# A decoder step whose three inner norms are applied after the first products of the next projection, and whose last two down groups are multiplied together

## The chip, the cores and the metric

One core of one Trainium2 chip runs one inference step of a two-layer decoder. The metric is the device time of one execution in microseconds; lower is better. All numbers are fp32; products run as pairs of `float32r` halves (below).

## The reference, cut to what matters

320 tokens (256 of a prompt, 64 of eight samples) pass through two layers of width 2048. Layer 0 has sparse attention with its own K/V, layer 1 dilated attention on a K/V that is projected once from the output of layer 0. After each mixer and each ConvFFN stands a layer norm over the 2048 features:

```python
x = LN(ALPHA * x + mixer(x))                # norm 1 (layer 0), norm 3 (layer 1)
x = LN(ALPHA * x + conv_ffn(x))             # norm 2 (layer 0), the output norm (layer 1)

def layer_norm(x, g, b):
    mu = x.mean(-1); var = square(x - mu).mean(-1)
    return (x - mu) * rsqrt(var + EPS) * g + b

def conv_ffn(h, state, w_up, conv_w, conv_b, w_down):
    gate, up = split(h @ w_up)              # 2048 -> 2 x 5504
    conv = conv_b + sum(ext[:, j:j + T] * conv_w[j] for j in range(3))
    return (silu(conv) * up) @ w_down       # 5504 -> 2048
```

What follows norms 1 and 3 is `h @ w_up`; what follows norm 2 is the shared `h @ w_kv` and then the query projection of layer 1. The change is about these three norms; the output norm isn't touched.

## The kernel before

**Layout.** Activations lie transposed: 16 tiles of 128 features (`d` = 0 to 15) by 320 tokens. R holds the residual, one `big` buffer of 128 x 5120; four such buffers exist.

**Products.** `Stream` walks one long list of weight chunks (4 feature tiles by 256 columns, 512 KB). Of each it issues the load on SP's queue three chunks ahead, splits it into `hi` on ScalarE (L82) and `lo` on VectorE (L84), two chunks ahead of use, and multiplies: for each feature tile three products of 128 x 128 weights by 320 columns, `hi*xh`, `hi*xl`, `lo*xh` (L123 to L125), accumulating in PSUM over 16 feature tiles. So a chunk of two column tiles is 24 products. A job is one or two column blocks; when a block is done its epilogue `epi_*` is called. Between chunks the `lanes` hand out steps of side work (attention, norms, tables) at given rates. The Tile scheduler then orders each engine's instructions, except those pinned by `keep_in_program_order`.

**The order of jobs.** ... wo of layer 0 (`epi_wo` adds each block to R, L502), the FFN, the shared K/V (`kvb`, `vb`), 24 query blocks (`qb`) with the attention of layer 1 beside them, wo of layer 1, the second FFN. An FFN works in groups of three or four tiles of the hidden width: up products of the first two tiles of a group (gate and up block each), the eight down jobs of the group before (`epi_down` adds to R, L586), up products of the rest. `epi_up` does the convolution (L554 to L556), silu and the product with up, and splits the result into the two halves of `H` (L567 on ScalarE, L568 on POOL). The last group's down jobs stand alone at the end.

**The norms before.** While the last job before a norm runs, `ln_tile` gathers sum and sum of squares (VectorE L352, POOL L353); `ln_end` adds the last two tiles (L361 to L363) and brings the sums across partitions by one-column products (L371). `ln_finish` forms rstd (L396 to L399), spreads mean and rstd over all partitions by small products (L388) copied by ScalarE (L392), and then, for each `d`: subtract the mean (POOL L409; VectorE L407 for the first two), scale (VectorE L410), write `xh` and R on ScalarE (L412, L413), `xl` on VectorE (L414). Norm 2 also stores R to DRAM from SP's queue (L417). `ln_prepare` then scales R for the next residual and shifts it (products L333, VectorE L339). The tables of layer 1's bias are added on POOL (L602 to L606) in a lane that starts with the first FFN.

## Time and profile before

| | us |
|---|---|
| median of 3 runs | 3305.78 |
| lowest and highest | 3305.71, 3306.69 |
| the profiled execution, own time | 3318.17 |
| its span, first to last instruction | 3316.0 |

TensorE is busy for 97% of the span by this profile, VectorE for 55%, ScalarE 41%, POOL 19%; the mean granted TensorE clock is 0.981. A busy TensorE here is one with a product in flight: products overlap, each stands in the trace with some 310 ns, and the interval between their starts is what counts. So the views that matter are those which count products in a stretch and those which tell what ended a stop.

### The profile page before, as it was taken

The page shows a single profiled execution, that of the slowest core. Times are in us where ns is not written, and L with a number is a line of the kernel's source. Part 1 is how long each engine was busy: PE and PEld are TensorE (multiplying, and loading weights), DVE is VectorE, ACT ScalarE, POOL GpSimd, SP SyncE. Part 2 cuts the span into 40 slices and gives each one's busy share as a digit, 9 for nine tenths or more (in the row PEclk, how much of TensorE's full clock was granted, in tenths as well). Part 3 has the DMA queues.
Part 4 walks back from the last instruction along what each step waited for, and adds up shares of the span by engine and source line. Part 5 has one row for each costly group of instructions (what it writes and reads, how often), then busy time and mean ns, then how long its engine had stood idle before and what let it go on. Part 6 is the DMA issues. An engine that isn't in the chain of part 4 may idle for free.

```text
span 3316.0 us, 58328 instructions
## 1 busy us (share of the span) xinstructions
PE 3226.7 (97%) x23574; PEld 3058.1 (92%) x23574; DVE 1832.6 (55%) x3170; ACT 1364.1 (41%) x2209; POOL 623.8 (19%) x820
## 2 busy tenths in 40 slices
PE   8999999999999999999999999999999999999998
PEld 7789766989999999999899898878999999999998
DVE  5748655675555555555744454554655555555556
ACT  4643445344333333333544343443443333333333
POOL 2223553550000000000401111111210000000003
PEclk8999999989999999999899999999899999999998
DMA  6655788535455555555475766766355545555554
GB/s 186 146 174 163 254 309 296 164 105 166 148 152 147 152 150 149 152 148 152 139 238 160 221 190 199 206 199 171 105 160 148 152 148 152 149 151 150 149 152 139
DMA packets 543249, 562.75 MB, mean 170 GB/s; under 512 B 24598, under 2 KB 520926, under 8 KB 538806
## 3 DMA queue, kind: packets, MB, share of 16 engines
q1 hardware_dynamic: 520692, 468.87, 48.5%
q0 software_dynamic: 19856, 85.75, 7.7%
q10 hardware_dynamic: 2432, 4.40, 0.4%
q8 instruction: 186, 3.05, 0.4%
q14 instruction: 83, 0.68, 0.1%
HBM read 542.14 MB, written 17.59 MB: 169 GB/s over the span
## 4 chain that ended last, share of the span: by engine, by line
PE 89%; DVE 4%; DMA 3%; ACT 1%; issue 1%; POOL 0%; SPq 0%; DVEq 0%; ACTq 0%; POOLq 0%
PE acc L123 26%; PE acc L124 26%; PE acc L125 26%; PE kt L1260 1%; DMA vtb<-in_cache_v_b_dram 1%; PE s L1057 1%; PE acc L1078 1%; PE s L1213 1%; PE oa L1129 1%; DMA kx<-in_cache_kidx_a_dram,i 1%; PE s L1160 1%; DVE hl L84 1%; PE ob L1303 1%; DVE R L410 1%; DVE w L852 0%
## 5 line engine op out<-in xcount | busy, mean ns | idle before, releaser
L84 DVE TENSOR_TENSOR hl<-raw,hl 128x1024 fp32r<-128x1024 f32 (+1 forms) x752 | 927.6, 1234 | 870.8 <-ACT hl L82 867.8
L82 ACT ACTIVATE hl<-raw 128x1024 fp32r<-128x1024 f32 (+3 forms) x770 | 804.3, 1045 | 1316.9 <-PE acc L125 1123.4
L123 PE MATMUL acc<-xh,hl 128*128 128x320 f32 (+1 forms) x4176 | 1316.5, 316 | 6.6 <-ACT xh L412 5.1
L124 PE MATMUL acc<-xl,hl 128*128 128x320 f32 (+1 forms) x4176 | 1299.9, 311 | 7.2 <-DVE xl L414 7.2
L125 PE MATMUL acc<-xh,hl 128*128 128x320 f32 (+1 forms) x4176 | 1297.9, 311 | 1.5 <-POOL hl L84 1.1
L123 PEld LDWEIGHTS acc<-xh,hl 128*128 128x128 f32 (+1 forms) x4176 | 790.1, 189 | 31.0 <-issue 20.8
L124 PEld LDWEIGHTS acc<-xl,hl 128*128 128x128 f32 (+1 forms) x4176 | 789.7, 189 | 15.2 <-DVE xl L414 12.5
L125 PEld LDWEIGHTS acc<-xh,hl 128*128 128x128 f32 (+1 forms) x4176 | 789.3, 189 | 6.0 <-issue 3.5
L124 PE MATMUL acc<-H,hl 128*128 128x320 f32 x1376 | 425.4, 309 | 1.1 <-POOL H L568 1.1
L123 PE MATMUL acc<-H,hl 128*128 128x320 f32 x1376 | 426.1, 310 | 0.0
L125 PE MATMUL acc<-H,hl 128*128 128x320 f32 x1376 | 425.3, 309 | 0.3 <-DVE hl L84 0.3
L124 PEld LDWEIGHTS acc<-H,hl 128*128 128x128 f32 x1376 | 258.3, 188 | 1.6 <-POOL H L568 1.6
L125 PEld LDWEIGHTS acc<-H,hl 128*128 128x128 f32 x1376 | 258.3, 188 | 0.6 <-DVE hl L84 0.6
L123 PEld LDWEIGHTS acc<-H,hl 128*128 128x128 f32 x1376 | 258.2, 188 | 0.1
L586 DVE TENSOR_TENSOR R<-R,acc 128x320 f32<-128x320 f32 x352 | 169.9, 484 | 122.0 <-PE acc L125 121.8
L551 POOL COPY gl<-E 128x2 f32<-128x2 f32 x86 | 24.8, 288 | 1039.4 <-ACT E L547 1039.4
L568 POOL TENSOR_TENSOR H<-h,H 128x320 fp32r<-128x320 f32 x86 | 106.1, 1235 | 452.5 <-ACT H L567 438.3
L123 PE MATMUL acc<-oh,hl 128*128 128x320 f32 x512 | 161.6, 317 | 0.5 <-ACT oh L994 0.5
L124 PE MATMUL acc<-ol,hl 128*128 128x320 f32 x512 | 160.0, 313 | 0.9 <-DVE ol L995 0.9
L125 PE MATMUL acc<-oh,hl 128*128 128x320 f32 x512 | 160.0, 313 | 0.0
L1150 POOL TENSOR_TENSOR bm<-tt,pmb 128x256 f32<-128x256 f32 x48 | 45.4, 971 | 327.1 <-DVE mxb L943 310.8
L123 PEld LDWEIGHTS acc<-oh,hl 128*128 128x128 f32 x512 | 96.7, 189 | 2.8 <-ACT oh L994 1.2
(391 smaller groups left out, 3176.8 us busy)
## 6 DMA issues: line engine op xcount, KB each, us to landing
raw<-in_ffn_w_up_dram SPq DMA_DIRECT2D x336, 512.0 KB, 3.8
raw<-in_ffn_w_down_dram SPq DMA_DIRECT2D x160, 512.0 KB, 3.6
raw<-in_b_w_q_dram SPq DMA_DIRECT2D x96, 512.0 KB, 3.6
raw<-in_a_w_in_dram SPq DMA_DIRECT2D x64, 512.0 KB, 5.0
krb<-in_cache_k_b_dram SPq DMA_DIRECT2D x96, 256.0 KB, 3.7
vtb<-in_cache_v_b_dram SPq DMA_DIRECT2D x92, 256.0 KB, 5.4
raw<-in_a_w_o_dram SPq DMA_DIRECT2D x32, 512.0 KB, 5.4
raw<-in_b_w_o_dram SPq DMA_DIRECT2D x32, 512.0 KB, 4.8
```

What stands on the lines that cost most here:

```text
L82: a = self.nc.scalar.activation(out=hl[:, 0, :m], in_=raw[:, :m], func=AF.Copy)
L84: b = eng.tensor_sub(hl[:, 1, :m], raw[:, :m], hl[:, 0, :m].bitcast(F))
L123: nc.tensor.matmul(acc[:cw, :NT], hi, xh, start=st, stop=False)
L124: nc.tensor.matmul(acc[:cw, :NT], hi, xl, start=False, stop=False)
L125: nc.tensor.matmul(acc[:cw, :NT], lo, xh, start=False, stop=sp)
L410: ve.scalar_tensor_tensor(r, r, lnp[:, d, which:which + 1], pr if d < 2 else rstd, OP.mult, OP.mult)
L568: ge.tensor_sub(lo, h, hi.bitcast(F))
L586: ve.tensor_add(r, r, acc[:, :NT])
L1057: te.matmul(p[32 * g:32 * g + 32, :], S["qsf"][:, b, 32 * g:32 * g + 32], kts[g], start=False, stop=True, tile_position=(0, 32 * g))
L1078: te.transpose(p[:, 128 * i:128 * i + 128], kr[:, o:o + 128], idf)
L1129: te.matmul(o[32 * g:32 * g + 32, 0:128], ptq[:, 128 * t + 32 * g:128 * t + 32 * g + 32], v, start=(q == 0 and t == 0), stop=(q == 4), til ...
L1150: ge.tensor_add(bm[:, g, :], tt, S["pmb"][:, g, :])
```

## The change

The three inner norms no longer stand between two projections.

- **Raw products.** While the projection before still runs, `scale_hi` (ScalarE) and `scale_lo` (VectorE) write the halves of g·R into `rh`, `rl`; `scale_gb` puts g and b themselves into two more columns, so these tiles have 322 columns (`NX`). The first jobs behind the norm (in an FFN the first group and the first two tiles of the second, 10 column tiles; behind norm 2 `kvb` and `vb`, 8) multiply these. `fix` then gives rstd·acc - mean·rstd·(W'g) and, as a bias, W'b.
- **Statistics in a lane.** `ln_stats` issues two sums (mean, mean square) and two spreads between raw products; the squares' sum moves from POOL to VectorE (`pool=False`).
- **Takeover.** `ln_rest` normalises R in place on VectorE at a low rate; `ln_conv` writes normalised halves over `rh`, `rl` as the last raw job lets go of them, and `ln_scale` (ScalarE) turns R into the next residual, which replaces `ln_prepare` for all but the first norm. `ln_store` stores norm 2's rows from ScalarE's queue, and `ot` is allocated after the first three query jobs.
- **Last two down groups as one**: eight jobs of eight feature tiles instead of two times eight jobs of four, after all up products.
- **Moved**: the bias tables' lane to behind the first down group; norm constants (`ffn_consts`) with g, b and the mean of b to wo block 4; the first K and V loads of layer 1's attention keep their program order.

Cut to its core (`fix`, the statistics and the two new lanes whole):

```diff
+NX = NT + 2
...
-                    nc.tensor.matmul(acc[:cw, :NT], hi, xh, start=st, stop=False)
-                    nc.tensor.matmul(acc[:cw, :NT], hi, xl, start=False, stop=False)
-                    nc.tensor.matmul(acc[:cw, :NT], lo, xh, start=False, stop=sp)
+                    nx = job.nx
+                    nc.tensor.matmul(acc[:cw, :nx], hi, xh, start=st, stop=False)
+                    nc.tensor.matmul(acc[:cw, :nx], hi, xl, start=False, stop=False)
+                    nc.tensor.matmul(acc[:cw, :nx], lo, xh, start=False, stop=sp)
...
+    def mv_r(k):
+        lo_upto(k + 1)
+        return S["rh"][:, k, :], S["rl"][:, k, :]
...
             if g == 0:
-                up(f0, n, True)
+                up(f0, n, True, True)
             else:
-                up(f0, 2, False)
-                down(g - 1, *starts[g - 1])
-                up(f0 + 2, n - 2, False)
-        down(len(starts) - 1, *starts[-1])
+                up(f0, 2, False, g == 1)
+                if g < end:
+                    down(g - 1, *starts[g - 1])
+                up(f0 + 2, n - 2, False, False)
+        down(end, starts[end - 1][0], starts[end - 1][1] + starts[end][1])
...
+    def scale_hi(d):
+
+        se.activation(out=S["rh"][:, d, 0:NT], in_=S["R"][:, d, :], func=AF.Identity,
+                      scale=lnp[:, d, S["which"]:S["which"] + 1])
+
+    def scale_lo(d):
+        ve.scalar_tensor_tensor(S["rl"][:, d, 0:NT], S["R"][:, d, :], lnp[:, d, S["which"]:S["which"] + 1],
+                                S["rh"][:, d, 0:NT].bitcast(F), OP.mult, OP.subtract)
...
+    def scale_gb(d, n):
+
+        gb = lnp.rearrange("p k (b w) -> p k b w", w=2)[:, d:d + n, :, S["which"]]
+        hi, lo = S["rh"][:, d:d + n, NT:NX], S["rl"][:, d:d + n, NT:NX]
+        ve.tensor_copy(hi, gb)
+        ve.tensor_sub(lo, gb, hi.bitcast(F))
...
+    def ln_stats(rate):
+
+        yield
+        yield
+        tk = S["rb"]
+        ve.memset(tk, 0.0)
+        pm, pv = ps("pm"), ps("pv")
+        for p, x in ((pm, S["s1"]), (pv, S["s2"])):
+            for t, n in TG:
+                te.matmul(p[:n, t:t + 1], x[:, 128 * t:128 * t + n], ones_d[:, 0:1], start=True, stop=True)
+        m, v, rs = tk[:, 0:3], tk[:, 4:7], tk[:, 8:11]
+        for t, n in ((slice(0, 2), 128), (slice(2, 3), 64)):
+            ve.tensor_scalar(m[:n, t], pm[:n, t], -1.0, None, OP.mult)
+            ve.tensor_copy(rs[:n, t], pv[:n, t])
+        ve.tensor_mul(v, m, m)
+        ve.tensor_sub(rs, rs, v)
+        se.activation(out=rs, in_=rs, func=AF.Sqrt, bias=epst)
+        ve.reciprocal(rs, rs)
+        ve.tensor_mul(m, m, rs)
+        yield
+        yield
+        for k, x in enumerate((m, rs)):
+            p = ps("mr")
+            for t, n in TG:
+                te.matmul(p[:, 128 * t:128 * t + n], x[:n, t:t + 1].to_broadcast([n, 128]), idf[:n, :n],
+                          start=True, stop=True)
+            se.activation(out=S["mr"][:, k, :], in_=p[:, :NT], func=AF.Copy)
+        S["norm"] = lanes.add(ln_rest(), rate)
+        yield
+
+    def ln_rest():
+
+        R, w = S["R"], S["which"]
+        for d in range(KD):
+            r, g = R[:, d, :], lnp[:, d, w:w + 1]
+            ve.scalar_tensor_tensor(r, r, g, S["mr"][:, 1, :], OP.mult, OP.mult)
+            ve.scalar_tensor_tensor(r, S["mr"][:, 0, :], g, r, OP.mult, OP.add)
+            yield
+
+    def ln_conv(scale):
+
+        R, w = S["R"], S["which"]
+        S["xh"], S["xl"] = S["rh"][:, :, 0:NT], S["rl"][:, :, 0:NT]
+        for d in range(KD):
+            r, b = R[:, d, :], lnp[:, d, 2 + w:3 + w]
+            se.activation(out=S["xh"][:, d, :], in_=r, func=AF.Identity, bias=b)
+            ve.scalar_tensor_tensor(S["xl"][:, d, :], r, b, S["xh"][:, d, :].bitcast(F), OP.add, OP.subtract)
+            if scale:
+                ln_scale(d)
+            yield
+
+    def ln_scale(d):
+
+        r, w = S["R"][:, d, :], S["which"]
+        se.activation(out=r, in_=r, func=AF.Identity, scale=ALPHA, bias=lnq[:, d, 2 + w:3 + w])
+
+    def ln_store():
+        for d in range(KD):
+            ln_scale(d)
+            if d % 4 == 3:
+                a = d - 3
+                se.dma_start(out=xs[1][:, a * NT:(a + 4) * NT],
+                             in_=S["R"][:, a:a + 4, :].rearrange("p k n -> p (k n)"))
+            yield
+
+    def fix(acc, t):
+
+        if S["stats"] in lanes.lanes:
+            lanes.drain(S["stats"])
+        uv = const.tile([128, 2], F, name="uv", tag="uv", bufs=4)
+        se.activation(out=uv, in_=acc[:, NT:NX], func=AF.Copy)
+        ve.tensor_mul(t, acc[:, :NT], S["mr"][:, 1, :])
+        ve.scalar_tensor_tensor(t, S["mr"][:, 0, :], uv[:, 0:1], t, OP.mult, OP.add)
+        return uv[:, 1:2]
...
+        if pool:
+            sq = S["fp"].tile([128, NT], F, name="sq", tag="sq", bufs=3)
+        else:
+            sq = ps("sq")[:, :NT]
         se.activation(out=sq, in_=R[:, d, :], func=AF.Square)
         ve.tensor_add(S["s1"], S["s1"], R[:, d, :])
-        ge.tensor_add(S["s2"], S["s2"], sq)
+        (ge if pool else ve).tensor_add(S["s2"], S["s2"], sq)
...
+        while S["nhi"] < min(2 * p + 2, 6 * p - 18):
+            scale_hi(S["nhi"])
+            S["nhi"] += 1
+        ln_pair(p, False)
...
+            if raw:
+                x = Fp.tile([128, NT], F, name="fx", tag="fx", bufs=4)
+                v = fix(acc, x)
...
+        if last and not l and p == 0:
+            S["which"] = 1
+            S["rh"], S["rl"], S["nlo"] = cols3(big("rh", FR), NX), cols3(big("rl", FR), NX), 0
...
+            if key == ("up", l, FGROUPS[0], 1):
+                run(key, 2)
+                if S["norm"] in lanes.lanes:
+                    lanes.drain(S["norm"])
+                lanes.add(ln_conv(True), 1.5)
+            if key[0] == "down" and key[2] == key[3] == 0:
+                ln_begin_sums()
+            if key == ("down", l, 1, 0) and l == 0:
+                lanes.add(gen_tables_b(), 0.5)
...
+    run(("vb", 0))
+    run(("vb", 1), 1)
+    if S["norm"] in lanes.lanes:
+        lanes.drain(S["norm"])
+    conv = lanes.add(ln_conv(False), 2.0)
+    run(("vb", 1))
     for hp in range(8):
         for g in range(3):
             run(("qb", hp, g))
+            if hp == g == 0:
+                lanes.drain(conv)
+                lanes.add(ln_store(), 1.0)
+        if hp == 0:
+            lanes.drain()
+            S["ot"] = cols3(big("ot"))
```

## Rows read from the trace of the kernel before

**Rows 1.** The page: the first engine's busy time, share of the span and instructions; and the shares by engine of the chain that ended last.
```profile
PE 3226.7 (97%) x23574; PEld 3058.1 (92%) x23574; DVE 1832.6 (55%) x3170; ACT 1364.1 (41%) x2209; POOL 623.8 (19%) x820
...
PE 89%; DVE 4%; DMA 3%; ACT 1%; issue 1%; POOL 0%; SPq 0%; DVEq 0%; ACTq 0%; POOLq 0%
```
**Rows 2.** The page's costliest groups: line, engine, operation, out<-in, shapes, count | busy us, mean ns of one | idle us of the engine just before them, and what ended it.
```profile
L84 DVE TENSOR_TENSOR hl<-raw,hl 128x1024 fp32r<-128x1024 f32 (+1 forms) x752 | 927.6, 1234 | 870.8 <-ACT hl L82 867.8
L82 ACT ACTIVATE hl<-raw 128x1024 fp32r<-128x1024 f32 (+3 forms) x770 | 804.3, 1045 | 1316.9 <-PE acc L125 1123.4
L123 PE MATMUL acc<-xh,hl 128*128 128x320 f32 (+1 forms) x4176 | 1316.5, 316 | 6.6 <-ACT xh L412 5.1
L124 PE MATMUL acc<-xl,hl 128*128 128x320 f32 (+1 forms) x4176 | 1299.9, 311 | 7.2 <-DVE xl L414 7.2
```
**Rows 3.** TensorE's work by stretches, only instructions that touch the split weights `hl` (that is, the products of L123 to L125): the stretch in us, its length, busy us (x products in it), granted clock, DMA share and GB/s. A steady stretch, then 40 us from the end of the last product before norms 1, 2 and 3.
```profile
800.00:1000.00 200.00, 200.00 (x1366) 1.00 0.51 151
692.45:732.45 40.00, 23.83 (x127) 0.70 0.24 65
1624.60:1664.60 40.00, 27.42 (x152) 0.74 0.55 156
2362.85:2402.85 40.00, 29.21 (x161) 0.79 0.24 73
```
**Rows 4.** The timeline at norm 2: start us, duration us, engine, line, operation, out<-in, count [idle before <- what ended it].
```profile
1624.27 0.31 PE L125 MATMUL acc<-H,hl 128*128 128x320 f32 x1
...
1632.46 0.44 ACT L392 ACTIVATE rstd<-rstd 128x320 f32<-128x320 f32 x1 [1.33 <-PE rstd L388]
...
1638.15 0.64 PE L124 MATMUL acc<-xl,hl 128*128 128x320 f32 x1 [2.58 <-DVE xl L414]
```
**Rows 5.** All engines by stretches: stretch, length, busy us (x instructions) of PE, PEld, DVE, ACT and POOL, granted clock, DMA share, GB/s. The three norms, the first FFN's start after norm 1, and a stretch after a stop in the attention of layer 1.
```profile
692.25:718.70 26.45, 20.22 (x77) 17.30 (x76) 19.89 (x26) 10.37 (x22) 17.88 (x17) 0.55 0.11 25
1625.00:1647.00 22.00, 17.21 (x68) 14.86 (x68) 16.25 (x23) 12.50 (x24) 15.79 (x18) 0.54 0.16 59
2362.00:2384.40 22.40, 18.52 (x83) 15.83 (x82) 18.18 (x27) 10.96 (x22) 14.06 (x14) 0.62 0.09 25
2206.90:2213.70 6.80, 4.74 (x19) 4.73 (x20) 0.54 (x1) 0.60 (x1) 0.00 (x0) 0.50 1.14 312
...
718.70:755.00 36.30, 36.30 (x249) 36.30 (x248) 30.77 (x58) 25.68 (x49) 7.04 (x11) 1.00 0.45 132
```
**Rows 6.** The timeline: small products at norm 3 at full clock (six one-column products, six of a spread), and a transpose between products at the end of the first FFN.
```profile
2365.31 0.81 PE L371 MATMUL pv<-ones_d,sq 128*64 128x1 f32 x6
...
2366.06 1.07 PE L388 MATMUL m<-idf,tk 64*128 64x64 f32 x6
...
1600.72 0.31 PE L125 MATMUL acc<-H,hl 128*128 128x320 f32 x1
1600.87 0.27 PE L618 MATMUL gt<-idf,gl 128*126 128x128 f32 x1
...
1601.13 0.30 PE L124 MATMUL acc<-H,hl 128*128 128x320 f32 x1
```
**Rows 7.** Single lines of code over the whole span: count, ns of one (least/median/most), first and last start in us, forms.
```profile
L586 DVE TENSOR_TENSOR R<-R,acc x352: 472/482/490, 786.4 to 3289.5; 128x320 f32<-128x320 f32 x176
L410 DVE SCALAR_TENSOR_TENSOR R<-R,lnp,rstd x48: 536/548/1226, 704.4 to 2392.7; 128x320 f32<-128x320 f32 x48
L555 DVE SCALAR_TENSOR_TENSOR c<-E,stc,c x86: 556/567/572, 738.3 to 3248.0; 128x336 f32<-128x336 f32 x86
L556 DVE SCALAR_TENSOR_TENSOR c<-E,stc,c x86: 555/569/572, 739.2 to 3248.6; 128x336 f32<-128x336 f32 x86
L396 DVE SCALAR_TENSOR_TENSOR tk<-tk x3: 161/163/164, 698.1 to 2364.9; 128x3 f32<-128x3 f32 x3
L412 ACT ACTIVATE xh<-R,lnp x48: 543/547/565, 704.9 to 2395.6; 128x320 fp32r<-128x320 f32 x48
L554 ACT ACTIVATE c<-E,stc x86: 663/667/673, 737.6 to 3247.1; 128x336 f32<-128x336 f32 x86
```
**Rows 8.** Two engines at once, in the timeline of norm 1 (POOL's table addition, VectorE's sum), the same sum at norm 3, and POOL's subtraction L568 over the span.
```profile
691.07 3.82 POOL L603 TENSOR_TENSOR sb<-trb,mk 16x1024 f32<-16x1024 f32 x1
...
692.62 2.62 DVE L362 TENSOR_TENSOR s<-s,R 128x320 f32<-128x320 f32 x1
...
2362.08 0.49 DVE L362 TENSOR_TENSOR s<-s,R 128x320 f32<-128x320 f32 x1
...
L568 POOL TENSOR_TENSOR H<-h,H x86: 879/1313/1998, 743.6 to 3260.7; 128x320 fp32r<-128x320 f32 x86
```
**Rows 9.** The timeline where the last down group of layer 0 begins.
```profile
1597.28 0.42 PE L124 MATMUL acc<-H,hl 128*128 128x320 f32 x1 [1.06 <-POOL H L568]
```
**Rows 10.** TensorE's waits over the span: who waited <- for whom: us in total, times, longest us.
```profile
PE kt L1260 <- DMA krb<-in_cache_k_b_dram: 5.8, 3, 5.3
```
**Rows 11.** The timeline at norm 1 and at norm 3: last product before, and the copy of the spread rstd.
```profile
692.11 0.31 PE L125 MATMUL acc<-oh,hl 128*128 128x320 f32 x1
...
703.89 0.44 ACT L392 ACTIVATE rstd<-rstd 128x320 f32<-128x320 f32 x1 [1.33 <-PE rstd L388]
...
2362.51 0.31 PE L125 MATMUL acc<-oh,hl 128*128 128x320 f32 x1
...
2368.72 0.44 ACT L392 ACTIVATE rstd<-rstd 128x320 f32<-128x320 f32 x1 [1.12 <-PE rstd L388]
```

More of the change, by code (lines that the diff above doesn't have):

```diff
@@ L272, in ffn_jobs, with up @@
         Wu, Wd = wview(ffn_w_up[l]), wview(ffn_w_down[l])
-        def up(f0, n, wide):
+        def up(f0, n, wide, raw):
+            mv, nx = (mv_r, NX) if raw else (mv_x, NT)
             cols = []
@@ new lines, in lo_upto, with gen_lo @@
+    def lo_upto(n):
+        while S["nlo"] < n:
+            d = S["nlo"]
+            if d % 4 == 0:
+                scale_gb(d, 4)
+            scale_lo(d)
+            S["nlo"] += 1
+    def gen_lo():
+        while S["nlo"] < KD:
+            lo_upto(S["nlo"] + 1)
+            yield
[27 more added lines that the diff above has]
+        yield
@@ L345, in ln_tile, with ln_begin_sums @@
+    def ln_begin_sums():
+        S["s1"] = S["lnpool"].tile([128, NT], F, name="s1", tag="s1")
+        S["s2"] = S["lnpool"].tile([128, NT], F, name="s2", tag="s2")
+    def ln_tile(d, pool):
         R, L = S["R"], S["lnpool"]
@@ L489, in out_end, with ln_pair, gen_lo_wo @@
             rest[n]()
-    def ln_pair(p):
-        if p == 7:
+    def ln_pair(p, pool, out=False):
+        if p == 7 and out:
             ln_end()
         else:
-            ln_tile(2 * p)
-            ln_tile(2 * p + 1)
+            ln_tile(2 * p, pool)
+            ln_tile(2 * p + 1, pool)
+    def gen_lo_wo():
+        for d in range(0, KD, 4):
+            yield
+            lo_upto(d // 2 + 2)
+            yield
     def epi_wo(l, p, accs):
@@ L528, in ffn_consts @@
         ve.tensor_copy(lnp, p[:, :64].rearrange("p (k c) -> p k c", c=4))
+        bm = S["fp"].tile([128, 4], F, name="bmean", tag="bmean")
+        ve.tensor_reduce(bm, lnp.rearrange("p k c -> p c k"), AX.X, OP.add)
+        p = ps("bm")
+        te.matmul(p[:, 0:4], ones_d, bm, start=True, stop=True)
+        ve.tensor_scalar(bm, p[:, 0:4], ALPHA, None, OP.mult)
+        ve.tensor_scalar(lnq, lnp, ALPHA, None, OP.mult)
+        ve.tensor_sub(lnq[:, :, 2:4], lnq[:, :, 2:4], bm[:, 2:4].unsqueeze(1).to_broadcast([128, KD, 2]))
+        yield
         for f0 in range(0, NF, 24):
@@ L537, in ffn_consts, with epi_up @@
         yield
-    def epi_up(l, f0, kind, accs):
+    def epi_up(l, f0, kind, accs, raw):
         Fp = S["fp"]
@@ L648, in ffn @@
             return
-        g = ln_finish(1, mode)
-        next(g)
-        return g
+        S["stats"] = lanes.add(ln_stats(0.8), 1.0)
+        lanes.add(gen_lo(), 1.0)
+        return True
     def epi_ki(accs):
@@ L906, in epi_kv @@
                 t = S["kvp"].tile([128, n], F, name="vt", tag=tag, bufs=bufs)[:, :NT]
-            se.activation(out=t, in_=acc[:, :NT], func=AF.Copy)
+            if kind in ("k", "v"):
+                se.activation(out=t, in_=acc[:, :NT], func=AF.Copy)
+            else:
+                x = S["lnpool"].tile([128, NT], F, name="fx", tag=("sh", "s1", "s2")[kv % 3])
+                v = fix(acc, x)
+                se.activation(out=t, in_=x, func=AF.Identity, bias=v)
             lanes.add(gen_kv(kind, kv, t), 1.0)
@@ L1561, in mixer_begin @@
             ge.dma_start(out=R[:, a:a + 1280], in_=xs[l][:, a:a + 1280])
-        return ln_prepare()
+            if l:
+                yield
+                yield
+        if l:
+            ln_begin_sums()
+        else:
+            yield from ln_prepare()
     def mixer_end(l):
@@ L1567, in mixer_end @@
         stn, lnn = ffn_begin(l)
+        S["which"] = 0
+        S["rh"], S["rl"], S["nlo"] = cols3(big("rh", FR), NX), S["ol"], 0
+        S["nhi"] = KD
         for p in range(8):
+            if p == 4:
+                consts = ffn_consts(stn, lnn)
+                next(consts)
+                lanes.add(consts, 0.5)
+                S["nhi"] = 0
+            if p == 7:
+                lanes.add(gen_lo_wo(), 1.0)
             if ("wo", l, p) in jobs:
                 run(("wo", l, p))
-            if p == 3:
-                lanes.add(ffn_consts(stn, lnn), 0.5)
-        g = ln_finish(0, "ffn")
-        next(g)
-        lanes.add(g, 1.0)
+        for x in ("oh", "ol"):
+            S.pop(x)
         norm = ffn(l, "xs" if l == 0 else "out")
         if norm:
-            S["norm"] = lanes.add(norm, 1.0)
             S["fp_end"] = pf.close
@@ L1583, in tile_yoco @@
     ln_begin(0)
-    lanes.add(mixer_begin(0), 1.0)
+    mix = mixer_begin(0)
+    next(mix)
+    lanes.add(mix, 1.0)
     mixer_end(0)
@@ L1590, in begin_b @@
     def begin_b():
-        lanes.drain(S["norm"])
+        if S["stats"] in lanes.lanes:
+            lanes.drain(S["stats"])
         S.pop("fp_end")()
@@ L1613, in tile_yoco @@
     run("kvb")
-    for j in range(2):
-        run(("vb", j))
-    lanes.drain()
-    S["ot"] = cols3(big("ot"))
-    S.pop("oh")
+    run(("vb", 0))
[4 more added lines that the diff above has]
+    run(("vb", 1))
     for hp in range(8):
```

132 lines of the change are left out of this document (54 added, 78 removed).

## The prediction

> **What bounds the kernel now.** I read the page first: TensorE is busy 97% of the span and holds 89% of the chain that ended last [rows 1], nearly all of it in the three product lines L123 to L125. VectorE and ScalarE are full of weight splits (L84, L82), but their idle time before a split ends on each other or on TensorE, so they follow [rows 2]. So only what stops or slows TensorE has a price. The page's groups show where it stops: the products' idle ends on `xh` (L412) and `xl` (L414), the two halves of a freshly normalised activation, and on little else [rows 2].
>
> The view by stretches, kept to instructions on the split weights, gives the size. In a steady stretch 200 us hold 1366 products, 0.1464 us each. The same view over 40 us from the end of the last product before each norm holds 127, 152 and 161 products; at 0.1464 us they would fill 18.6, 22.3 and 23.6 us. **Each norm therefore costs 21.4, 17.7 and 16.4 us, 55.5 in all** [rows 3]. The timeline of the second one shows two parts: the sums, the root and the two spreads last from the last product at 1624.27 to the copy of rstd at 1632.46, then the products creep behind L410 to L414 until the first `xl` product at 1638.15 [rows 4]. And the granted clock is at 0.54 to 0.62 in these stretches, that is, mostly at 1.2 GHz and back at 2.4 after, so the products that do run there take nearly twice their time [rows 5].
>
> **Part 1: raw products first.** The next projection starts on g·r (halves `rh`, `rl`) instead of the normalised tile, with g and b as two extra columns; `fix` applies rstd and mean to the finished accumulator. The first raw product needs only d=0 to 3, and these are scaled while the projection before still runs; d=14 and 15 are wanted three weight chunks (72 products, 10.5 us) after the last one. The 55.5 us go, and with them the half clock and both spreads' place in the path.
>
> What TensorE gets back: two sums (mean and square; before there were four groups) and two spreads a norm. Three plain f32 products stand in the trace as six instructions; at full clock such a sum took 0.81 us and a spread 1.07 [rows 6], so 2 x 0.81 + 2 x 1.07 = 3.8. One transpose between products stretched two intervals, 0.293 us, to 0.41 [rows 6], so I add 0.12 for each of the four change-overs: 4.3 a norm, **13 us back**. (They ran in the norms before, too, but inside the 55.5.) The mean of b, one small product for two of the norms, is below 0.3 us.
>
> The two extra columns: 28 column tiles (10 in each FFN, 8 in the shared K/V) of 48 products, 1344 in all. The trace has no 322-column product; a column can cost nothing (if an interval is set by the weight load) or at most 0.1464/320 us = 0.46 ns, so 0 to 1.2 us. I take **1.2**, since the interval is close to the columns' time.
>
> **Part 2: the work beside it.** This is VectorE's bill, and the cover I rely on. From the first norm to where the raw products end there are 18 full weight chunks, 63.3 us of products. VectorE's list: 18 splits at 1.23; two R additions and four sum additions at 0.48 to 0.49 (the squares' sum moves here from POOL); eight `rl` at 0.55 and the g, b columns, 5.2; the statistics, ten at 0.16; the normalising in place, 32 at 0.548; five gate tiles at 2.17 (two for `fix`, two for the convolution); three up tiles at 1.8 [rows 2, 6, 7]. Sum 22.1 + 2.9 + 5.2 + 1.6 + 17.5 + 10.9 + 5.4 = **65.6 us against 63.3**. That is level. A split is made two chunks (7 us) ahead, and before the change VectorE was busy 30.8 of 36.3 us beside products that never stopped [rows 5]. At the second norm four chunks (14.1 us) meet 4.9 of splits, 7.0 of normalising and 2.9 of `fix` and copies, 14.8 us; then the takeover has four `xl` a chunk, 1.2 + 2.2 = 3.4 against 3.5, and nothing between it and the query products. In the FFNs eight down jobs (21 us) lie between takeover and use, so it is covered there. The first sum comes after 36 raw products, 5.3 us; VectorE has by then two R additions, four sums, a split and a few `rl` to do, some 5 us, so a wait there is small. I allow 1 us at each norm and 2 more at the second: **5 us**; the bounds are 0 (backlog within the 7 us lead) and 25 (rival A).
>
> Beside this row stands a rule that speaks against the change. In the trace, the sum addition L362 took 2.62 us beside a POOL addition of 3.82 and 0.49 where POOL was idle; L410's 0.548 became 1.226 at most [rows 7, 8]. The Trainium skill ("SBUF — State Buffer", Who interferes with whom) says that a VectorE instruction with two SBUF inputs and a GpSimd instruction that reads SBUF exclude each other for the whole instruction; the trace agrees. By that rule the three `H` subtractions of a raw stretch would add up to 3 x 1.3 us to the list above and the waits would be some 3 us more an FFN; taking the squares' sum off POOL works the other way.
>
> ScalarE's list is shorter: scaling between 0.547 (one pointer, L412) and 0.667 (two, L554), 16 a norm, replaces nothing late; `xh` and the residual scaling keep the two 0.547 passes of L412 and L413 and run in the down jobs or the query products [rows 7]. Removed besides: three `shift` products and 48 scalings (L339), beside other work, at nothing. The store of the normalised rows leaves SP's queue, where it stood among weight loads, for ScalarE's; no product waited for that in the trace, so nothing. The tables' additions on POOL are moved behind the first FFN norm: they stretched L362 by 2.1 us at the first norm, which is inside the 21.4. Holding the first K and V loads of the last attention in order: zero, their wait is another unit's.
>
> **Part 3: the last two down groups as one.** Sixteen R additions a layer go, all hidden. The products on the last `H` waited 1.06 us for POOL's subtraction in layer 0 [rows 9]; with the group before multiplied first, that is covered: **1.1 us gained**. At the very end R gets 7 us a pair instead of 3.5; the tail after the last product is as before.
>
> **Sum:** 55.5 + 1.1 - 13 - 1.2 - 5 = 37.4 us. The profiled execution took 3318.2 us (span 3316.0), 12 above the median of the runs shown; the norms lie inside the span, so I take the sum off the median: 3305.8 - 37.4 = **3268**. With no waits 3263; with twice mine 3273.
>
> **Rival A: VectorE becomes the bound at the norms.** The sums above are level or 2 to 5% over, and a wait of some size costs more than itself: after the 5.3 us wait for `krb`, 6.8 us ran at a granted clock of 0.50 [rows 5, 10], 3.4 us lost. If each norm keeps a 5 us wait and one such fall, 3 x 8.4 = 25 us go back instead of 5: 3288. For: 65.6 against 63.3, the locks of [rows 8]. Against: the 7 us lead, 85% load without a stop [rows 5]. It decides from a backlog of more than two chunks.
>
> **Rival B: the statistics hold TensorE's queue.** The sums and spreads stand in order between raw products. If each waits for its whole chain, the stop from last product to the copy of rstd (11.8, 8.2 and 6.2 us, together 26) [rows 4, 11] is paid as before, the clock falls as before, and most of the other 29 of the 55.5 follows: the gain is gone, 3305. For: that is the order of today. Against: products stand between, two steps apart, and they wait for nothing of the chain. This is also the case in which the change doesn't do what it says.
>
> **Rival C: slower.** Rows of `rh`, `rl`, `oh`, `ol` are now 322 long, so rows start at any multiple of 8 bytes, and the normalised tiles keep that stride: the up products, the shared K/V, the queries and the output projections read them. Together about 12,500 products (8256 FFN, 384 K/V, 2304 query, 1536 output) leave today's 1280-byte rows. If an off-grid start cost TensorE's read as much as 16 columns (7.3 ns), 91 us would come on top: 3268 + 91 = 3359. It decides from 37.4 us / 12,480 = 3 ns a product, 2% of the interval. Against: VectorE reads the gate one and two elements off at 567 and 569 ns, as much as 336 columns should take after 548 for 320 [rows 7]. No row has TensorE off the grid; that keeps the case open.
>
> **How the numbers follow.** Forecast 0.74; A 0.14; B 0.04; C 0.07; 0.01 for something slower that I don't see. For the range: 3257 is the forecast without waits (3263), without a price for the two columns (1.2), and with the sums and spreads at a third less, since they may overlap their neighbours (4 to 5); 3292 takes in A and 4 us for the locks of [rows 8]. B and C stay outside. About 0.2% (6.6 us) is what a measurement of this kernel can tell from no change: faster 0.88 (forecast and A), same 0.04 (B), slower 0.08.
>
> **What would show it.** Right: the view by stretches on the split weights shows over 230 products in the 40 us after each last product, at granted clock 1.00; no idle above 2 us ended by the raw halves or by the takeover; VectorE at 90% or more in these stretches; products of the steady stretches at 0.146 us as now. A shows as idle ended by VectorE's split or by the normalising, with the clock at 0.5 behind it; B as idle before the one-column sums; C as a longer interval in the later up products. I am wrong if the three stretches are clean and the time still isn't down by 30.

## The result and the profile after

| | median us | against the kernel before on the same chip |
|---|---|---|
| kernel before | 3306.24 (6 runs) | 1 |
| changed kernel | 3275.18 (6 runs) | 0.9903, 95% interval 0.9892 to 0.9914 |
| changed kernel, run again | 3275.05 (4 runs) | 0.9906, 0.9891 to 0.9921 |

One of the first six runs of the changed kernel was disturbed (7826 us) and stays out of the ratio. The change brings 31 to 32 us (28 to 36 by the interval of the first six); the forecast was 37.4, to 3268. The profiled execution took 3271.64 us, its span 3269.6.

The page of the changed kernel, to be held against [rows 1, 2]: busy time by engine, and two groups of products (they are now L125 to L127; the splits are L83 and L85).

```profile
PE 3201.6 (98%) x23524; PEld 3038.7 (93%) x23524; DVE 1862.4 (57%) x3341; ACT 1385.2 (42%) x2279; POOL 526.5 (16%) x727
...
L125 PE MATMUL acc<-rh,hl 128*128 128x320 f32 (+1 forms) x3648 | 1143.2, 313 | 0.0
L127 PE MATMUL acc<-rh,hl 128*128 128x320 f32 (+1 forms) x3648 | 1130.6, 310 | 0.6 <-DVE hl L85 0.6
```

The 6 to 7 us of idle time that two of the product lines of before had, ended by `xh` and `xl` [rows 2], are gone. (The trace keeps a buffer's first name: the normalised halves stand under `rh` and, at the two FFN norms, `ol`.) The view by stretches on the split weights, as in [rows 3]: a steady stretch, then 40 us from the end of the last product before norms 1, 2 and 3; columns as there.

```profile
800.00:1000.00 200.00, 200.00 (x1361) 1.00 0.53 156
684.35:724.35 40.00, 36.90 (x247) 1.00 0.36 102
1601.75:1641.75 40.00, 36.35 (x236) 1.00 0.59 171
2326.85:2366.85 40.00, 36.90 (x247) 1.00 0.36 103
```

Where 127, 152 and 161 products stood, there are 247, 236 and 247, and the granted clock is 1.00 where it was 0.70 to 0.79. At 0.1464 us a product the norms now cost 40 - 36.2, 40 - 34.6 and 40 - 36.2, that is 3.8, 5.4 and 3.8, **13.1 us in all** for 55.5. The steady stretch, though, holds 1361 products where it held 1366. That is the part of the result that the forecast doesn't have.

What stands between the raw products at norm 1, in the timeline: two sums and one pair of spreads (12 instructions).

```profile
689.58 0.81 PE L393 MATMUL pm<-ones_d,s 128*64 128x1 f32 x6
690.33 0.81 PE L393 MATMUL pv<-ones_d,s 128*64 128x1 f32 x6
694.73 2.07 PE L408 MATMUL mr<-idf,rb 64*128 64x64 f32 x12
```

They take 3.7 us together, and at norms 1 and 3 they are nearly all of the 3.8. VectorE in the raw stretches (all engines by stretches, columns as in [rows 5]; norm 1 and norm 2):

```profile
684.35:747.65 63.30, 63.07 (x424) 62.13 (x424) 51.56 (x98) 31.36 (x56) 7.64 (x14) 1.00 0.48 139
1603.00:1660.00 57.00, 56.91 (x386) 55.65 (x385) 45.73 (x84) 27.54 (x49) 4.81 (x9) 1.00 0.55 162
```

51.6 us of work in 63.3, 81%, where the forecast had 65.6. And the only waits of products that the view of waits shows from norm 1 to the end of its takeover (684 to 790 us; who waited <- for whom: us in total, times, longest us):

```profile
PE acc L127 <- DVE hl L85: 0.2, 1, 0.2
PE acc L125 <- DVE R L696: 0.2, 1, 0.2
```

Some of the loss there shows only in the count. The 60 us behind the 40 hold 400 products in each FFN (first and second line); 409 and 410 is what the same stretch of the kernel before holds with rows of the same length (run `before_rows322`, below). So 9 or 10 products, 1.4 us, go at each takeover, 2.8 in all.

```profile
724.35:784.35 60.00, 59.56 (x400) 1.00 0.56 163
2366.85:2426.85 60.00, 59.44 (x400) 1.00 0.55 168
```

### The profile page after: what moved, and what is told of

Read it like the earlier page. It is cut to its first block, busy times and chain, and to the rows that moved or that the text cites. A ratio compares the mean times of both kernels' runs of the same rounds, so it can differ in the third digit from the quotient of the medians.

```text
span 3269.6 us, 58311 instructions
## 1 busy us (share of the span) xinstructions
PE 3201.6 (98%) x23524; PEld 3038.7 (93%) x23524; DVE 1862.4 (57%) x3341; ACT 1385.2 (42%) x2279; POOL 526.5 (16%) x727
## 4 chain that ended last, share of the span: by engine, by line
PE 87%; DVE 6%; DMA 3%; ACT 2%; issue 1%; SPq 0%; POOL 0%; DVEq 0%; ACTq 0%; POOLq 0%
PE acc L125 25%; PE acc L127 25%; PE acc L126 25%; PE kt L1388 1%; DVE hl L85 1%; PE s L1183 1%; PE oa L1255 1%; DMA vtb<-in_cache_v_b_dram 1%; PE acc L1204 1%; PE s L1341 1%; DMA kx<-in_cache_kidx_a_dram,i 1%; PE ob L1431 1%; PE s L1286 1%; DMA krb<-in_cache_k_b_dram 1%; DVE R L419 0%
## 5 line engine op out<-in xcount | busy, mean ns | idle before, releaser
L85 DVE TENSOR_TENSOR hl<-raw,hl 128x1024 fp32r<-128x1024 f32 (+1 forms) x752 | 923.3, 1229 | 829.5 <-ACT hl L83 828.0
L83 ACT ACTIVATE hl<-raw 128x1024 fp32r<-128x1024 f32 (+3 forms) x770 | 803.7, 1045 | 1242.4 <-PE acc L127 1024.9
L125 PE MATMUL acc<-rh,hl 128*128 128x320 f32 (+1 forms) x3648 | 1143.2, 313 | 0.0
L127 PE MATMUL acc<-rh,hl 128*128 128x320 f32 (+1 forms) x3648 | 1130.6, 310 | 0.6 <-DVE hl L85 0.6
L126 PE MATMUL acc<-ol,hl 128*128 128x320 f32 (+1 forms) x3264 | 1014.0, 311 | 0.9 <-DVE ol L1121 0.9
L125 PEld LDWEIGHTS acc<-rh,hl 128*128 128x128 f32 x3648 | 687.5, 188 | 10.7 <-issue 9.9
L127 PEld LDWEIGHTS acc<-rh,hl 128*128 128x128 f32 x3648 | 688.1, 189 | 4.2 <-issue 3.1
L126 PEld LDWEIGHTS acc<-ol,hl 128*128 128x128 f32 x3264 | 617.3, 189 | 2.5 <-issue 1.2
L125 PE MATMUL acc<-H,hl 128*128 128x320 f32 x1376 | 425.9, 310 | 0.4 <-DVE R L696 0.3
L127 PE MATMUL acc<-H,hl 128*128 128x320 f32 x1376 | 424.9, 309 | 0.0
L126 PE MATMUL acc<-rl,hl 128*128 128x320 f32 (+1 forms) x896 | 277.8, 310 | 0.0
L125 PEld LDWEIGHTS acc<-H,hl 128*128 128x128 f32 x1376 | 258.4, 188 | 1.4 <-ACT R L438 0.8
L127 PEld LDWEIGHTS acc<-H,hl 128*128 128x128 f32 x1376 | 258.2, 188 | 0.2
L696 DVE TENSOR_TENSOR R<-R,acc 128x320 f32<-128x320 f32 x320 | 153.1, 483 | 105.8 <-PE acc L127 105.6
L125 PE MATMUL acc<-xh,hl 128*128 128x320 f32 (+1 forms) x528 | 170.1, 322 | 1.5 <-ACT hl L83 1.5
L126 PEld LDWEIGHTS acc<-rl,hl 128*128 128x128 f32 x896 | 169.1, 189 | 1.9 <-issue 1.2
L127 PE MATMUL acc<-xh,hl 128*128 128x320 f32 (+1 forms) x528 | 164.7, 312 | 1.5 <-POOL hl L85 1.1
L126 PE MATMUL acc<-xl,hl 128*128 128x320 f32 (+1 forms) x528 | 165.3, 313 | 0.0
```

Of the source, the lines that this page charges most:

```text
L83: a = self.nc.scalar.activation(out=hl[:, 0, :m], in_=raw[:, :m], func=AF.Copy)
L85: b = eng.tensor_sub(hl[:, 1, :m], raw[:, :m], hl[:, 0, :m].bitcast(F))
L125: nc.tensor.matmul(acc[:cw, :nx], hi, xh, start=st, stop=False)
L126: nc.tensor.matmul(acc[:cw, :nx], hi, xl, start=False, stop=False)
L127: nc.tensor.matmul(acc[:cw, :nx], lo, xh, start=False, stop=sp)
L696: ve.tensor_add(r, r, acc[:, :NT])
```

## Experiments

Two theories were to be told apart throughout. **Mine:** the gain is the lead of raw products over the statistics; some of it goes back in longer products, because the normalised halves now stand in rows of 322 numbers. **Rivals:** the gain comes from cheaper statistics and needs no lead; the longer interval has another cause; VectorE is the narrow place. Runs 1, 2 and 8 shared a chip with another run of the changed kernel:

> The changed kernel itself, as the reference for the runs beside it. Expected 3272 to 3278 us, some 32 us under the kernel before, with products on the normalised halves at 147.1 to 147.5 ns and products on the hidden layer at 146.7 in its trace.

That held (3275.05 us). "Over after" is the difference of the ratios to the kernel before, taken by 3306; runs on one chip are compared by their medians too.

**1. Rows of 320 again: `packed`.**

```diff
-        S["xh"], S["xl"] = S["rh"][:, :, 0:NT], S["rl"][:, :, 0:NT]
+        S["xh"], S["xl"] = cols3(S["rhf"]), cols3(S["rlf"])
...
```

(`rhf` and `rlf` are the buffers of the raw halves, whole.)

> The changed kernel, but the normalised halves xh and xl are written as rows of 320 numbers again at the takeover; the raw halves and the attention's output keep rows of 322. Theory (rows that start off the grid cost TensorE's read): some 9,600 products by 0.4 to 0.8 ns come back, 4 to 8 us under the changed kernel, and the products on the normalised halves stand at 146.7 ns. Rival (the longer interval has another cause, such as the load of the memory by the other engines): the same time as the changed kernel within 2 us, and the same 147.1 to 147.5 ns.

Measured 3271.45 us (ratio 0.9889, 0.9874 to 0.9904) beside 3275.05 for the changed kernel: 3.6 us less. It has the lowest median of this study, but the intervals of the two overlap; the trace decides (the views below run 4).

**2. Rows of 322 in the kernel before: `before_rows322`.**

```diff
+NX = NT + 2
...
-        return big_p.tile([128, 5120], dt, name=name, tag="big")
+        t = big_p.tile([128, KD * NX], dt, name=name, tag="big")
+        return t if name in ("xh", "xl") else t[:, 0:5120]
...
-        S["xh"] = cols3(big("xh", FR))
-        S["xl"] = cols3(big("xl", FR))
+        S["xh"] = cols3(big("xh", FR), NX)
+        S["xl"] = cols3(big("xl", FR), NX)
```

> The kernel before, with nothing changed but that the normalised halves xh and xl of the three norms stand in rows of 322 numbers (10,944 products read them). Theory (the rows): 4 to 9 us over the kernel before, and these products at 147.1 to 147.5 ns where they are 146.7 now. Rival (the interval has another cause in the changed kernel): 0 to 1 us.

Measured 3312.37 us (1.0019, 1.0010 to 1.0028), 6.4 over the kernel before on that chip, as the theory had it.

**3 and 4. Rows of 320 that begin 2 numbers (`before_shift2`) or 8 numbers (`before_shift8`, OFF = 8) into the buffer, in the kernel before.**

```diff
+OFF = 2
...
+        t = big_p.tile([128, 5136], dt, name=name, tag="big")
+        return t[:, OFF:OFF + 5120] if name in ("xh", "xl") else t[:, 0:5120]
...
```

> The kernel before, with the normalised halves xh and xl in rows of 320 numbers as they were, but begun two numbers (8 bytes) into their buffers: every row starts off the grid by the same 8 bytes. Theory A (the start of a row off the grid costs): the products on them leave 146.67 ns for 147 or more, 5 us or more over the kernel before. Theory B (what costs is that the starts differ from row to row, 8 bytes further at each): 146.67 ns as before, 0 us.

> The same with the halves begun eight numbers (32 bytes) into their buffers. Theory A with a grid of 32 bytes or less: 146.67 ns, 0 us. Theory A with a grid of 64 bytes: 147 ns or more, as with 8 bytes. Theory B: 146.67 ns.

Measured 3326.63 us (1.0061, 1.0044 to 1.0078) and 3312.56 us (1.0017, 1.0007 to 1.0026). The view by stretches on the split weights, one stretch of 700 us in each FFN (850 to 1550, 2500 to 3200), for the kernel before:

```profile
850.00:1550.00 700.00, 700.00 (x4775) 1.00 0.51 150
2500.00:3200.00 700.00, 700.00 (x4774) 1.00 0.51 150
```

the changed kernel:

```profile
850.00:1550.00 700.00, 700.00 (x4758) 1.00 0.50 151
2500.00:3200.00 700.00, 700.00 (x4759) 1.00 0.51 152
```

`packed`:

```profile
850.00:1550.00 700.00, 700.00 (x4773) 1.00 0.49 151
2500.00:3200.00 700.00, 700.00 (x4771) 1.00 0.49 153
```

`before_rows322`, with its three norms (40 us from the last product) and the 60 us behind the first of these stretches:

```profile
850.00:1550.00 700.00, 700.00 (x4759) 1.00 0.49 149
2500.00:3200.00 700.00, 700.00 (x4763) 1.00 0.49 150
...
684.91:724.91 40.00, 27.15 (x149) 0.74 0.24 70
1616.87:1656.87 40.00, 27.41 (x165) 0.83 0.55 171
2352.46:2392.46 40.00, 29.17 (x161) 0.79 0.25 73
...
724.91:784.91 60.00, 60.00 (x409) 1.00 0.49 149
```

and `before_shift2`, with its three norms and then those of `before_shift8`:

```profile
850.00:1550.00 700.00, 700.00 (x4717) 1.00 0.49 148
2500.00:3200.00 700.00, 700.00 (x4744) 1.00 0.49 149
...
685.72:725.72 40.00, 22.25 (x124) 0.74 0.22 63
1629.14:1669.14 40.00, 29.07 (x162) 0.79 0.59 176
2366.41:2406.41 40.00, 29.20 (x160) 0.79 0.24 73
...
684.30:724.30 40.00, 22.78 (x132) 0.79 0.24 69
1618.62:1658.62 40.00, 29.07 (x162) 0.79 0.57 178
2356.06:2396.06 40.00, 29.19 (x163) 0.79 0.24 73
```

The reader should see that in these runs the count follows the rows. 700 us by the count is 146.6 ns a product with rows of 320 (before, `packed`) and 147.1 with rows of 322, in either kernel; with every row 8 bytes off it is 148.4 and 147.6. `before_shift8` holds 4760 in both stretches, 147.1: 32 bytes off costs as well, which rules out a grid of 32 bytes or less; how wide it is stays open. So a row that starts off the grid (elsewhere than the 1280-byte rows of before) lengthens the product that reads it, and it isn't the change of start from row to row (theory B of run 3 falls). These counts mix in the products on the hidden layer, whose rows didn't change and whose intervals stand at 146.6 to 146.7 ns in the first FFN of all these runs. Taken apart by the starts in the trace, the products on `xh` and `xl` stand at 146.7 ns with rows of 320 and at 147.4 (first FFN) and 147.2 (second) with rows of 322, 0.7 and 0.5 more. If the nth product of one trace is set beside the nth of another, `packed` gains 2.6 us on the changed kernel from product 2500 to 8000 and 2.1 us from 12,500 to 18,000 (the two FFNs): **4.7 us**; `before_rows322` loses 2.8 and 2.0 in the same places.

**5 to 7. The lead taken away.** `held_by_stats` makes the low raw halves from d=4 on wait for rstd; `held_at_once` and `held_hard` have `d == 1` in that line, and `mv_r` below belongs to `held_hard` alone (it issues the statistics whole; in the other two the steps between them are taken out of `ln_stats`):

```diff
     def scale_lo(d):
+        if d == 4 and not S["which"]:
+            ve.tensor_copy(S["rl"][:, d, 0:2], S["mr"][:, 1, 0:2])
...
     def mv_r(k):
+        if k and not S["which"] and S["stats"] in lanes.lanes:
+            for _ in S["stats"][0]:
+                pass
+            lanes.lanes.remove(S["stats"])
...
```

> The changed kernel, with the norm's statistics issued without products between their steps, and the low raw halves of d=4 and after at the two FFN norms written only once rstd is spread (one copy of two numbers from the spread into the tile, which the later pass overwrites). So TensorE has 24 raw products of cover, 3.5 us, for a chain of 6 to 12 us. Theory (what buys the gain is the lead of raw products over the statistics): a stop of 3 to 8 us at each of the two norms and a lower clock behind it, +10 to +25 us over the changed kernel. Rival (the gain came from the cheaper statistics themselves, two sums for four, and the lead buys nothing): 0 to 2 us.

> The changed kernel with a harder hold than the run before: the low raw halves of d=1 and after at the two FFN norms are written only once rstd is spread (same copy of two numbers), so TensorE meets the hold after some 3 products of each chunk at its first column tile and not after 50. Theory (the lead of raw products is what buys the gain): a stop of 6 us or more at each of the two norms, with the clock at half behind it, +15 to +30 us over the changed kernel, most of what these two norms gained. Rival (the cheaper statistics buy it, two sums and two spreads in an already loaded stretch): +2 to +6 us.

> The changed kernel with a hold that stands: at the two FFN norms the statistics are issued whole after the first three raw products, and the low raw halves of d=1 and after are written only once rstd is spread. The run before this one (hold at d=1) had its copy issued ahead of the statistics and held nothing, so this one puts the question again. Theory (the lead of raw products buys the gain): a stop of 6 us or more at each of the two norms with a lower clock behind it, +12 to +30 us over the changed kernel. Rival (the cheaper statistics buy it): +2 to +6 us.

`held_by_stats`: 3284.98 us, 0.9911 (0.9893 to 0.9929), some 2 us over after: the theory's 10 to 25 didn't come. The reason is the cover: TensorE still had 52 raw products to run ahead of the hold, 7.6 us at 0.1464 and not the 24 and 3.5 us that I had written, and only the last 1.1 us of the chain stuck out (the one wait of the view: `acc` on DVE, 1.1 us, at each of the two norms). So this run doesn't take the lead away and decides nothing between the two. `held_at_once`: 3273.93 us, 0.9900 (0.9883 to 0.9916): no difference, but its copy was issued ahead of the statistics and read the old rstd, so it held nothing. It says one thing: without products put between their steps by hand the statistics cost no more. `held_hard` put the question again: 3300.04 us, **0.9955 (0.9941 to 0.9969)**, 16 us over after, inside the theory's 12 to 30. TensorE in its two held norms (by stretches, split weights) and its waits at the first:

```profile
701.13:741.13 40.00, 31.53 (x199) 0.87 0.30 86
2353.52:2393.52 40.00, 31.52 (x200) 0.87 0.30 86
...
PE mr L415 <- DVE rb L409: 1.7, 1, 1.7
PE acc L126 <- DVE ol L367: 1.6, 1, 1.6
PE pv L400 <- DVE rb L403: 0.2, 1, 0.2
...
706.98 3.60 PE L415 MATMUL mr<-idf,rb 64*128 64x64 f32 x12 [1.65 <-DVE rb L409]
```

Only 16 raw products run before the hold. The next one starts 8.2 us later; of these 3.5 us are named as waits, and in the others TensorE has only the small products of the statistics. Against 247, 48 and 47 products are missing, 7 us at each norm. Part of that is the clock, 0.87 in the mean: the last row has the spreads at 3.60 us where they took 2.07 above. So the lead is worth 14 us by the counts, 16 by the time, and 16 products of it, 2.3 us, were left. The two norms lost 40 - 149 x 0.1464 = 18.2 and 16.4 us in `before_rows322`, 10.9 and 10.7 here, 3.8 and 3.8 after. **Both theories hold a part**: about half of what these norms gained is the lead, and the other half stays nearly without it. That this half is the shorter chain ahead of rstd, and that no product waits for `xh` and `xl` any more, is argued and not shown: no run takes these two apart.

**8. The last two down groups apart again: `down_apart`.**

```diff
-                if g < end:
-                    down(g - 1, *starts[g - 1])
+                down(g - 1, *starts[g - 1])
...
-        down(end, starts[end - 1][0], starts[end - 1][1] + starts[end][1])
+        down(end, *starts[end])
```

> The changed kernel, with the last two down groups of each FFN multiplied one after the other again. Theory: the wait for the last hidden tile comes back in layer 0, 1.1 us, and R is added twice more a layer beside other work, so +1 us, at most +2. Rival: one down group fewer between the last gate and the next norm also means fewer epilogues of VectorE in the raw stretch, so that undoing it brings waits at the takeover: +3 to +6 us.

Measured 3281.79 us (0.9933, 0.9919 to 0.9946) beside 3275.05: 6.7 us by the medians, 8.9 by the ratios. The rival was right, at norm 2. Its 40 us on the split weights, the waits of TensorE there, and ScalarE's statistics:

```profile
1601.45:1641.45 40.00, 31.94 (x192) 0.96 0.56 162
...
PE acc L125 <- DVE R L695: 2.6, 2, 2.0
PE acc L125 <- ACT hl L83: 1.5, 1, 1.5
...
1614.54 0.30 ACT L399 ACTIVATE rb<-rb,epst 128x3 f32<-128x3 f32 x1 [3.78 <-DVE rb L398]
1617.96 0.44 ACT L409 ACTIVATE sel<-mr 128x320 f32<-128x320 f32 x1 [3.12 <-PE mr L407]
```

44 products fewer than 236, 6.4 us, and 1.6 us before that at the last `H` (nth product against nth). The last down job is the one that runs into norm 2. With one group in it, each pair of blocks lasts 3.5 us, and VectorE has two R additions, four sums, a split and two `rl` to do in that time. Back to back these passes start 0.40 (additions, sums), 1.14 (split) and 0.46 us (`rl`) apart, so 6 x 0.40 + 1.14 + 2 x 0.46 = 4.5 us. It falls behind: the first raw products wait 2.6 us until R additions are done, ScalarE stands idle 3.8 us before the root and 3.1 before the spread, and the next weight split comes behind these. With two groups a pair lasts 7 us and none of TensorE's waits is in the view. This reading rests on the waits; no run gave VectorE the time in another way.

**9. More work for VectorE: `vector_more`.**

In `ln_rest`, for each `d`:

```diff
+            for _ in range(2):
+                ve.scalar_tensor_tensor(r, r, 1.0, r, OP.mult, OP.max)
```

> The changed kernel, with two more VectorE passes of about 0.55 us over each of the 16 residual rows in the normalising (each takes the larger of a number and itself, so nothing of the result changes): 17.5 us more of VectorE in each raw stretch, 51.6 + 17.5 = 69 us of work beside 63 us of products. Theory of the prediction (VectorE was already level with the products at 65.6): the extra 17.5 come out as waits nearly whole, 10 us or more at a norm and a lower clock behind them, +30 us and more. Rival (VectorE is only at 81% in these stretches, as the trace after shows, and has a lead of 7 us besides): 0 to 8 us in all.

Measured 3292.13 us (0.9938, 0.9915 to 0.9960): 11 us over after, between the two. The nth products put it at 4.4, 1.0 and 4.9 us at norms 1, 2 and 3. The stretch of norm 1, TensorE's waits from there to 800 us, and the added passes (count, ns of one: least/median/most, first and last start in us):

```profile
692.40:755.70 63.30, 61.56 (x412) 60.36 (x412) 57.46 (x114) 29.79 (x53) 6.91 (x12) 1.00 0.43 126
...
PE acc L127 <- DVE hl L85: 2.2, 3, 1.0
PE acc L125 <- ACT hl L83: 1.3, 1, 1.3
PE acc L125 <- DVE R L698: 0.5, 3, 0.2
...
L422 DVE SCALAR_TENSOR_TENSOR R<-R x96: 473/484/491, 707.5 to 2416.0; 128x320 f32<-128x320 f32 x96
```

The added passes stand with 0.48 us each, not 0.55, and start 0.40 us apart, so they are 12.9 us of VectorE at a norm and not the 17.5 that was expected. Of these 4.4 to 4.9 come out at an FFN norm, as short waits at full clock, so VectorE takes up some 8 us there; in the 63.3 us themselves it is busy 5.9 more (57.46 against 51.56), and the rest falls behind them. Rival A was further off than the forecast had it.

**10. The squares' sum on POOL again: `squares_on_pool`** (`ln_pair(p, True)` for `ln_pair(p, False)`, at two places).

> The changed kernel, with the sum of the squares on POOL's engine again, as before the change, which shuts VectorE's two-input passes out while it runs. Theory (the lock delays the statistics and VectorE's list by 3 to 8 us a norm, and the raw stretch has that to spare): 0 to 2 us, with the sums standing later between the raw products. Rival (the lock decides whether the takeover is in time): +3 to +10 us, as waits ended by VectorE.

Measured 3277.63 us (0.9889, 0.9872 to 0.9906): no loss. The lock is in its trace, POOL's sum and a `rl` pass of VectorE at norm 1:

```profile
691.16 1.80 POOL L476 TENSOR_TENSOR s<-s,sq 128x320 f32<-128x320 f32 x1 [0.83 <-ACT sq L474]
692.14 1.17 DVE L361 SCALAR_TENSOR_TENSOR ol<-R,lnp,rh 128x320 fp32r<-128x320 f32 x1
```

1.17 us for a pass that takes 0.55 alone. The Trainium skill ("SBUF — State Buffer", Who interferes with whom) has the two exclude each other; the trace agrees, and with some 8 us to spare (run 9) it costs nothing that the time shows. The 3 us more an FFN that the forecast worked out from this rule don't stand in the trace either: the loss behind an FFN norm is 1.4 us with everything in it.

**11. The first K and V loads of the last attention free: `loads_free`** (the argument that holds them in order left out at two places).

> The changed kernel, with the first K and V loads of the last attention free to be issued early again. Theory: no product waits for their place, 0 within 2 us. Rival: they go out between weight loads of the layer before and hold a weight chunk up, +3 us or more, seen as a wait of a product or a split on the load.

Measured 3280.63 us on the chip of runs 5, 9 and 10, 0.9899 (0.9882 to 0.9916): no difference, as forecast.

## Why the forecast came out as it did

The mechanism and the sign were right, and so was most of the size, in part because two errors partly cancel: the waits were put too high, and the longer products at nothing. Of the forecast's signs, three came true (over 230 products in each 40 us, the clock at 1.00, no wait above 2 us) and two didn't: VectorE is busy 81% in the raw stretch and not 90%, and the steady products left 146.6 ns for 147.1, the sign of rival C. By the steps of the forecast:

| term | forecast | shown |
|---|---|---|
| what the three norms cost before | 55.5 | 55.5 in that execution; 50.4, 54.7 and 53.1 in runs 2, 3 and 4 |
| sums, spreads, columns and waits that stay | -13 - 1.2 - 5 | -13.1 in the 40 us, -2.8 behind the two FFN norms |
| wait for the last `H` | +1.1 | +1.6 |
| longer products (rows of 322) | 0 | -4.7 |
| sum | 37.4 | from 50.4 - 15.9 + 1.6 - 4.7 = 31.4 to 55.5 - 15.9 + 1.6 - 4.7 = 36.5; measured 31 to 32 |

**The 55.5 is the highest of four, but not far off.** Four traces hold the three norms as they were before. At 0.1464 us a product they cost 55.5, 50.4 (18.2 + 15.8 + 16.4, run 2), 54.7 and 53.1 us (runs 3 and 4, 21.8 and 20.7 of it at norm 1). Run 2 is the odd one at norm 1, and the reason lies in the lock that the forecast names: in the profiled execution of before, VectorE's last sum over R (L362) fell beside POOL's table addition and took 2.62 us [rows 8], and the stop from the last product to the copy of rstd was 11.8 us [rows 11]. In run 2 the addition was over by then:

```profile
684.60 0.31 PE L126 MATMUL acc<-oh,hl 128*128 128x320 f32 x1
...
684.99 0.49 DVE L364 TENSOR_TENSOR s<-s,R 128x320 f32<-128x320 f32 x1
...
693.06 0.44 ACT L394 ACTIVATE rstd<-rstd 128x320 f32<-128x320 f32 x1 [1.33 <-PE rstd L390]
```

So that stop was 8.5 us, 3.3 shorter, about as much as 18.2 lies below 21.4. At norm 2 the stops differ by only 0.5 us (8.2 and 7.7), but the mean clock of the 40 us behind them is 0.74 and 0.83. The step "I take the sum off the median" therefore gained too much by 1 to 5 us, and not by the 12 us that this execution was above the median: the last product before norm 1 starts at 692.11 us in it [rows 11] and at 684.60, 685.41 and 683.99 in runs 2 to 4, so 7 or 8 of the 12 lie ahead of the first norm. For the same reason the two profiled executions can't be set against each other: 8.1 of the 46.4 us between their spans lie there.

**Rival C, put at 0 or 91 us, happened in small.** The step that failed is the price of an off-grid row: the forecast took 0 from VectorE, which reads the gate one and two elements off at no cost [rows 7]. TensorE isn't VectorE: it pays 0.5 to 0.7 ns a product on such rows, 4.7 us in the two FFNs by runs 1 and 2. (Some of the shared K/V, query and output products read such rows too; they aren't in this number.) The rival's own point, 3 ns a product, is far off.

**VectorE's list was over-stated.** 65.6 us forecast, 51.6 in the trace. About half of the 14 us is work that fell elsewhere: only 3 of 8 `rl`, one of two R additions and three of five gate convolutions stand in the stretch. The other half is the way of adding up: a pass stands in the trace with 0.55 us, but the next one starts 0.46 us after it, so two of the normalising take 1.01 us (here of the second run of the changed kernel), and durations added up give 58.0 us in this stretch for 51.6 of busy time.

```profile
698.88 1.01 DVE L419 SCALAR_TENSOR_TENSOR R<-R,lnp,sel 128x320 f32<-128x320 f32 x2 [0.36 <-ACT sel L410]
```

The waits came to 2.8 us, not 5; run 9 shows the spare time.

**Norm 2 was rightly the tight one, but for a reason that the forecast priced at 1.1 us.** It called the merged down groups a matter of the last `H`; run 8 shows that they are worth 7 to 9 us, 6.4 of them at norm 2; by its waits that is because they give VectorE 7 us a pair instead of 3.5 right ahead of the raw products. The forecast said that of the end of the kernel and didn't apply it to the norm.

**Rival B** has its price now: 14 to 16 us for two norms, not the whole gain, even where the statistics are issued as one block.

Not settled: where between 31.4 and 36.5 the sum of the terms lies in a typical execution, and so whether a term is still missing; what makes the 1.4 us behind each FFN norm in single steps (the views name 0.4 of it), and why the same 8-byte offset costs more in the first FFN (148.4 ns) than in the second (147.6).

## What to carry to other kernels

To move a norm behind the product that follows it pays for its half-clock stretch as well as for its idle time, but what lies in the last job before the norm decides whether the raw products can start at once: give VectorE there twice the time for each block before counting what comes after. Where a tile gets extra columns, write the part that many products read back into rows on the old grid; here that gave 4.7 us by the trace and 3.6 by the medians. When the work of an engine is added up from a trace, take the time from one start to the next and not the durations. And when a term is read from one execution far above the median, look where in that execution the excess lies, and read the term in a second one.

## What the runs showed of the hardware

- A product of 320 columns took 146.7 ns where rows start every 1280 bytes, 147.1 on average with rows of 1288 bytes, 147.1 with all rows 32 bytes off and 147.6 to 148.4 with all rows 8 bytes off (stretches of 700 us, products on the hidden layer included). VectorE and ScalarE wrote rows of 1288 bytes in the same time: ScalarE's scaling into `rh` took 550 ns, against 547 for `xh`, and VectorE's pass into `rl` 545, against 548 for L410 [rows 7].
- The half clock after nearly the same stop lasts differently from execution to execution: at norm 2, behind stops of 8.2 and 7.7 us, 152 and 165 products stand in 40 us, at a mean clock of 0.74 and 0.83 (before, `before_rows322`).
- A stop of 8.2 us between two raw products, filled by the small products of the statistics and 3.5 us of waits (`held_hard`), cost 7 us against the changed kernel, with the clock at 0.87 in the mean of 40 us; waits of 4.0 us in `vector_more`, none above 1.3, cost no clock (1.00 throughout).
- VectorE's last sum over R took 2.62 us beside POOL's table addition [rows 8] and 0.49 where the addition was over (`before_rows322`); the stop from the last product to the copy of rstd at norm 1 was 11.8 and 8.5 us.
